# A streaming encoder layer with two kinds of attention: another order of its eight units, a seventeenth weight buffer, and norms of two tiles taken alone

## The chip, the core and the metric

The kernel runs on one core of a Trainium2 chip, in one launch. The metric is the device time of that launch in microseconds, the median of several runs. The core has a matrix engine (PE, or TensorE), a vector engine (DVE, VectorE), a scalar engine for activation functions and scaled copies (ACT, ScalarE), a general engine (POOL, GpSimd) and a queue engine that starts DMA transfers (SP). Each engine works through its own instructions in order and waits on semaphores for the others.

## The reference, cut to what matters

One layer is computed for a prompt of 2048 frames of width 1024 and for 8 running streams ("samples") with 16 new frames and 512 cached frames each:

```python
h, gate = adaln_modulate(x, c, norm_g, w_ada, b_ada)           # rms norm, scale and shift
qa, ka, va, za, qb, kb, vb, zb, ga, gb = split(h @ w_in)       # 512 columns each, ga and gb 1024
qa, ka = rope(qa, pos), rope(ka, pos)
# A, "diff attention", 4 heads of two 64-wide components, mask by chunks of 64 frames
p = softmax(where(mask, q @ k.T / 8, -inf));  oa = (p[0] - lam * p[1]) @ v
# B, "stick breaking", 8 heads of 64, strictly causal
log_a = log_sigmoid(z) + reverse_cumsum(log_sigmoid(-z)) - log_sigmoid(-z);  ob = exp(log_a) @ v
# merge
oa = rms_norm(oa, subln_g) * (1 - lam_init)                    # over each head's 128 columns
ya = (oa * silu(za)) @ w_branch_a
yb = (ob * silu(zb)) @ w_branch_b
y = rms_norm(x + gate * ((sigmoid(ga) * ya + sigmoid(gb) * yb) @ w_out), final_g)
```

The outputs are y for prompt and samples, and the new keys and values of both attentions.

## The kernel before

**Tiles and units.** The prompt is 16 tiles of 128 frames (t = 0 to 15, NT = 16); the 8 x 16 sample frames are one more tile, t = NT. The attention is cut into eight *units*, each with 128 columns of q, k, v and z: four units of kind 0, "A", one head of diff attention each, and four of kind 1, "B", two heads of stick breaking each. In this text A0 is the first A unit, B3 the last B unit. Unit u has h = u // 2 and kind = u % 2, so they run A0 B0 A1 B1 A2 B2 A3 B3.

**What a unit does.** `prepare_unit(u)` loads the unit's columns of w_in, takes their sum of squares, and splits them, scaled, into two fp16 numbers each (high and low part). An A unit holds four weight buffers of 4 KB per partition for that, a B unit eight, since the columns of the merge gates ga and gb are projected in B units (`GATES`). The buffers come from a list `free`. Then, for each tile: `project` does 24 matmuls of 512 columns for q, k, v and z (L423), and in B units 24 more for the gate columns (L495); `transpose_qk` turns q and k; `scores` does the score matmuls (L647, L648, and L651 for a mask), up to 512 keys to a bank of PSUM. An A tile then takes a softmax for its two components (`softmax_pair`): maximum and scaled copy on DVE (L545), Exp on ScalarE, difference of the two on DVE (L594), a cast on ScalarE (L287), the rest on DVE (L292). A B tile takes Sigmoids on ScalarE, scans on DVE (L607, L655), products on POOL (L629), a cast on ScalarE (L561) and the rest on DVE (L562). A DMA transposes the weights, and PE multiplies them with the values (L702 to L704 for A, L706 and L707 for B). For A units a sum of squares of each output tile goes into `osums`, for the norm of oa. The outputs go to DRAM (o_d), as do z (z_d) and the gate columns (g_d). The work of the sample tile is cut into pieces (`spare`) that are strewn over the following units.

**What sets the order.** The program writes the order by hand: `line` is the list of all projection pieces; while it emits the attention of step n, `take` and `interleave` add projection pieces so that projections stay LEAD = 5.0 tiles ahead of attention, weighed by `duration(t)`. The multiplication with the values comes PV_LAG = 2 steps after the scores, and `ripe` holds some of these back at the start of a unit and for tile 15 of an A unit. `prepare_unit(u + 1)` is called at the last step of unit u - 1 and its pieces (`back`) run beside the attention of unit u, so at that time the buffers of a unit in use, of one being used up and of one in preparation are taken. A tile scheduler then orders the instructions of each engine. All Exp and Sigmoid calls go through `act` (L120), which keeps them in program order on ScalarE; where the function changes, ScalarE loads another table (ACT_TABLE_LOAD, shown under the same line).

**The last unit and the last phase.** During unit 7 the weights of the branches are cut (`branch_weight`), and near its end `early_work` does the first part of the last phase: `inputs` of tiles 0 and 1 and the branches of tile 0. The last phase does for each tile: `inputs(t)` loads o, z and the gates, multiplies o by z on POOL (L1230), by Sigmoid of z and, for the A half, by the norm of each head on DVE; takes Sigmoids of the gates; then sum of squares, scale and split. `branches` (L1262) multiplies with the two branch weights and the gates on DVE (L1264) and POOL (L1266), and `output` (L1399) with w_out; its product m is made on DVE (L1403) and added to x on POOL (L1407). The norms of all 16 prompt tiles are one tile `orms` of 64 columns (16 tiles x 4 heads), computed once by twelve small DVE instructions in `rsqrt` (L233 to L246) when `early_work` first calls `inputs`.

Of the kernel before, what the change touches and what calls it, by code (L numbers as in the profile page):

```python
# [16 lines left out]
F32 = mybir.dt.float32  # L17
# [8 lines left out]
P = 128  # L26
# [6 lines left out]
NT = SEQ // P  # L33
# [24 lines left out]

GATES = [(u // 2 * 512, u % 2 * 512) for u in range(8)]

# [50 lines left out]
def layer_kernel(ctx: ExitStack, tc: tile.TileContext, a: dict):  # L111
# [59 lines left out]
    ps = ctx.enter_context(tc.tile_pool(name="ps", bufs=2, space=bass.MemoryType.PSUM))  # L171
    tiny = ctx.enter_context(tc.tile_pool(name="tiny", bufs=6))
    unit = ctx.enter_context(tc.tile_pool(name="unit", bufs=2))
# [130 lines left out]
    def prepare_unit(u):  # L304


        h, kind = u // 2, u % 2
        U = dict(h=h, kind=kind, u=u, w=[], wg=[], bufs=[])
# [434 lines left out]
    def sample(U, dec, fixed):  # L743
# [77 lines left out]
        def values():  # L821
            po = bank("s")
            n = 128 // heads
            for c in range(heads):
                cols = slice(c * n, c * n + n)
                T.matmul(po[:, cols], wn[:, c, :], box["s"][:, 256 + c * n : 256 + c * n + n], start=True, stop=False)
                for r in range(2):
                    for j in range(4):
                        for i in range(4):
                            T.matmul(po[i * 32 : i * 32 + 32, cols], wz[c][:, j, 2 * i + r, :], box[nv, i][:, r * 4 + j, cols],  # L830
                                     start=False, stop=(r == 1 and j == 3))
            o = dec.tile([P, P], F32, tag="o", name="o", bufs=2)
            S.activation(out=o, in_=po[:, 0:P], func=AF.Identity, scale=box["jobs"][0]["r"] if kind == 0 else 2.0 ** -STICK)
# [90 lines left out]
    def ripe(k, n):  # L924

        t = steps[k][1]
        if n >= len(steps) or n <= len(P0_STEPS) or 3 < t < NT and not (t == NT - 1 and steps[k][0] % 2 == 0):
            return True
        return sum(duration(t) for _, t in steps[k + 1 : n]) >= (1.0 if t == NT - 1 else 1.5)
# [261 lines left out]
    (gts,) = buffers_of_4k("gt", 1)  # L1191
    free += buffers_of_4k("wb", 8)
    whole = sum(duration(t) for _, t in steps)
# [12 lines left out]
    L = {}  # L1206
# [8 lines left out]
    def inputs(t):  # L1215
# [8 lines left out]
        begun.append(t)  # L1224
        r = L["orms"][:, 4 * t : 4 * t + 4] if t < NT else rsqrt(osums[:, NT, :], 4, P, tiny, "rA")
        for n in range(2):
# [79 lines left out]
    def early_work():  # L1306
# [4 lines left out]
        def first(t):  # L1311
            if "orms" not in L:
                L["orms"] = rsqrt(osums[:, 0:NT, :].rearrange("p t h -> p (t h)"), 4 * NT, P, con, "orms")
            states[t] = inputs(t)
            if t == tiles[0]:
                turned(states[t])
# [43 lines left out]
    with ExitStack() as c2:  # L1360
# [17 lines left out]
        def gate_rows(i, n):  # L1378

            pg = bank("t")  # L1380
            gsm = s2.tile([P, 512], F32, tag="sg", name="gsm", bufs=2)
            load(out=gsm[0:9, :], in_=gate_d[:, n * 512 : (n + 1) * 512])
# [3 lines left out]
        def output(t, st):  # L1386
            box = {}

            def half(j):
# [7 lines left out]
                for yi, wi in ((0, 0), (0, 1), (1, 0)):  # L1397
                    for k in range(KT):
                        T.matmul(po, st["y"][:, yi * 8 + k, :], wo[j * 4 + k // 2][:, wi, k % 2, :], start=(n == 0), stop=(n == 3 * KT - 1))  # L1399
                        n += 1  # L1400
                m = s2.tile([P, 512], F32, tag="sg", name="m", bufs=2)
                if t < NT:
# [77 lines left out]
```

## Time and profile before

| | |
|---|---|
| runs | 2287.53, 2288.26, 2289.09 us; median 2288.26 |
| the profiled execution | 2285.48 us; its span 2283.7 us |
| instructions | 40470 |
| PE busy | 2085.1 us, 91% of the span |
| PE weight loads busy | 1110.4 us, 49% |
| DVE busy | 1611.5 us, 71% |
| ScalarE busy | 1482.6 us, 65% |
| POOL busy | 688.1 us, 30% |
| last value matmul of the last unit | 1763.3 us |

Times within the profiled execution count from the start of its span. A busy engine is one with an instruction under way; matmuls overlap, so a group's busy time is not the sum of single durations. Rows name the line of the code, the engine, the operation and the tiles it writes and reads, with buffer numbers left out. "L120" is the helper `act`, so its rows are told apart by their tiles. "idle before" is time in which the engine had nothing to do ahead of these instructions, with what ended it.

### The profile page before, as it was taken

Reading aid. Unit: us, or ns where it says so; the run is one execution under the profiler, and the core shown is the slowest. Engines: PE = TensorE matmul, PEld = TensorE weight load, DVE = VectorE, ACT = ScalarE, POOL = GpSimd, SP = SyncE. Lnnn points to the kernel's source line nnn. Section 1 sums busy time; section 2 is a strip of 40 time slices with the busy share of each in tenths; the row PEclk is TensorE's granted clock in tenths of the full one; section 3 lists DMA queues with packets and bytes.
Section 4 is the critical chain, followed back from the end, with each engine's and each line's share of the span. In section 5 each row is a group of like instructions: output and inputs, shape, how many; then the busy total and the mean of one; then the engine's idle time right before and its main releaser. Section 6 shows DMA issues by size and latency. Waiting matters only on the chain. (4 is left out here: it accounts for less than half of the span.)

```text
span 2283.7 us, 40470 instructions
## 1 busy us (share of the span) xinstructions
PE 2085.1 (91%) x14478; PEld 1110.4 (49%) x14478; DVE 1611.5 (71%) x3507; ACT 1482.6 (65%) x2952; POOL 688.1 (30%) x559
## 2 busy tenths in 40 slices
PE   4997999999999999899999989999986799888997
PEld 2554554555555455455545555555543444444443
DVE  4668767789875778987577898776777656565554
ACT  3877677787876777786677777666776544444431
POOL 1522012355301335530032553012344232232321
PEclk7999999999999999999999999999997899999998
DMA  8667658697875778876566886757687989788652
GB/s 295 211 212 187 163 131 220 148 221 155 206 169 124 170 154 199 177 179 131 128 172 142 204 183 154 153 140 163 151 179 173 295 228 262 202 220 211 188 150 65
DMA packets 763754, 411.92 MB, mean 180 GB/s; under 512 B 524986, under 2 KB 708586, under 8 KB 763040
## 3 DMA queue, kind: packets, MB, share of 16 engines
q1 hardware_dynamic: 762474, 408.86, 72.6%
q8 instruction: 113, 1.85, 0.3%
q14 instruction: 89, 0.73, 0.1%
q10 hardware_dynamic: 1078, 0.48, 0.1%
HBM read 211.53 MB, written 72.91 MB: 125 GB/s over the span
## 5 line engine op out<-in xcount | busy, mean ns | idle before, releaser
L423 PE MATMUL ps_mm<-wb,hs 128*128 128x512 f16 x1836 | 460.7, 382 | 0.6 <-DVE v L292 0.5
L629 POOL TENSOR_TENSOR sc_p<-sc_p,sc_n 128x1024 f32<-128x1024 f32 (+8 forms) x160 | 278.1, 1742 | 459.2 <-DVE sc_n L607 451.6
L423 PEld LDWEIGHTS <-hs 128*128 128x128 f16 x2928 | 256.1, 98 | 226.9 <-issue 6.8
L607 DVE TENSOR_TENSOR_SCAN sc_n<-ps_s,sc_n,zero_t 128x512 f32<-128x512 f32 x192 | 245.3, 1278 | 64.4 <-ACT ps_s L120 62.2
L423 PE MATMUL ps_mm<-wa,hs 128*128 128x512 f16 x1092 | 279.4, 380 | 0.0
L647 PE MATMUL ps_s<-k,qst 128*128 128x512 f16 (+3 forms) x640 | 225.9, 354 | 38.3 <-DVE sc_n L607 30.1
L120 ACT ACTIVATE sc_p<-ps_s,usc 128x512 f32<-128x512 f32 (+3 forms) x320 | 202.0, 631 | 85.8 <-PE ps_s L648 55.1
L495 PE MATMUL ps_mm<-wa,hs 128*128 128x512 f16 x1020 | 257.0, 379 | 0.0
L562 DVE TENSOR_TENSOR sc_n<-sc_p,sc_n 128x1024 f16<-128x1024 f32 (+7 forms) x160 | 197.9, 1242 | 41.3 <-ACT sc_n L561 41.2
L648 PE MATMUL ps_s<-k,qst 128*128 128x512 f16 (+3 forms) x640 | 226.2, 354 | 0.0
L1399 PE MATMUL ps_o<-wo,wb 128*128 128x512 f16 x816 | 199.5, 401 | 24.7 <-DMA wb<-wa 22.0
L706 PE MATMUL ps_o<-v,wt 128*128 128x128 f16 x1008 | 175.6, 226 | 27.6 <-DMA wt<-sc_n 27.5
L495 PEld LDWEIGHTS <-hs 128*128 128x128 f16 x1632 | 140.2, 98 | 119.0
L120 ACT ACTIVATE ps_s<-ps_s,usc 128x512 f32<-128x512 f32 (+3 forms) x320 | 193.7, 605 | 0.0
L561 ACT CAST sc_n<-sc_p 128x1024 f16<-128x1024 f32 (+7 forms) x160 | 138.5, 870 | 49.2 <-POOL sc_p L629 49.1
L707 PE MATMUL ps_o<-v,wt 128*128 128x64 f16 x1008 | 158.5, 198 | 0.0
L495 PE MATMUL ps_mm<-wb,hs 128*128 128x512 f16 x612 | 155.9, 379 | 0.0
L706 PEld LDWEIGHTS <-wt 128*128 128x128 f16 x1008 | 99.2, 102 | 102.7 <-DMA wt<-sc_n 38.0
L1399 PEld LDWEIGHTS <-wb 128*128 128x128 f16 x816 | 82.1, 102 | 130.4 <-DMA wb<-wa 26.1
L457 POOL TENSOR_TENSOR rot<-pr,rope 128x256 f32<-128x256 f32 x68 | 63.1, 928 | 247.1 <-ACT pr L437 193.3
L437 ACT ACTIVATE pr<-ps_mm,usc 128x512 f32<-128x512 f32 (+1 forms) x136 | 86.5, 636 | 67.4 <-PE ps_mm L423 67.1
L545 DVE TENSOR_SCALAR_CACHE_REDUCE sc_n<-ps_s,usc 128x512 f32<-128x512 f32 (+3 forms) x148 | 99.0, 669 | 42.4 <-PE ps_s L648 28.2
(336 smaller groups left out, 4346.7 us busy)
## 6 DMA issues: line engine op xcount, KB each, us to landing
hs<-hT_d SPq DMA_DIRECT2D x122, 512.0 KB, 4.2
g_d<-gt SPq DMA_DIRECT2D x68, 256.0 KB, 3.4
out_dram<-pr SPq DMA_DIRECT2D x204, 64.0 KB, 1.8
wa<-g_d SPq DMA_DIRECT2D x25, 512.0 KB, 6.7
wide<-in_w_ada_dram SPq DMA_DIRECT2D x12, 1024.0 KB, 8.4
wa<-in_w_in_dram SPq DMA_DIRECT2D x44, 256.0 KB, 4.7
z_d<-pr SPq DMA_DIRECT2D x136, 64.0 KB, 2.7
o_d<-o SPq DMA_DIRECT2D x136, 64.0 KB, 2.7
```

Source lines behind the costliest of these rows:

```text
L120: i = S.activation(**kw)
L423: T.matmul(box["p"], box["h"][:, hi, k, :], U["w"][k][:, wi, :], start=(n == 0), stop=(n == 3 * KT - 1))
L495: T.matmul(box["g"][:, 0:gw], box["h"][:, hi, k, :], U["wg"][k // per][:, k % per, wi, :], start=(j == 0), stop=(j == 3 * KT - 1))
L561: S.copy(out=hi, in_=src)
L562: V.tensor_tensor(out=lo, in0=src, in1=hi, op=ALU.subtract)
L607: V.tensor_tensor_scan(out=dst[:, lo : lo + n][:, ::-1], data0=src[:, 0:n][:, ::-1], data1=zero_t[:, 0:1].to_broadcast([P, n]), initial=fi ...
L629: G.tensor_tensor(out=p[:, 0:m], in0=p[:, 0:m], in1=n[:, 1 : m + 1], op=ALU.mult)
L647: T.matmul(p[:, 0:n], qst[:, c, :], kk[:, c, 0:n], start=True, stop=False)
L648: T.matmul(p[:, 0:n], qst[:, 2 + c, :], kk[:, c, 0:n], start=False, stop=not diag)
L706: T.matmul(po[:, c * P : (c + 1) * P], wt[:, wj, :], vt[:, c, :, :], start=first, stop=False)
L707: T.matmul(po[:, c * P : c * P + 64], wt[:, nb + wj, :], vt[:, c, 0, :], start=False, stop=last)
L1399: T.matmul(po, st["y"][:, yi * 8 + k, :], wo[j * 4 + k // 2][:, wi, k % 2, :], start=(n == 0), stop=(n == 3 * KT - 1))
```

## The change

The order of the units is written out. It is A0 B0 A1 B1 B2 A2 B3 A3, so two B units are neighbours in the middle and the last unit is an A unit. A ninth buffer in the pool `wb` gives seventeen weight buffers in all, as B1 and B2 hold eight each at the same time. To make room for it, three small pools lose a buffer each: `tiny` (small columns) 6 to 5, the samples' output `o` 2 to 1, and m in `output` 2 to 1 (tag "sg", which the samples' gate row `gsm` shared; that row now uses a tile of the tag "dks"). As the last unit is now an A unit, the sums of squares that `orms` needs come last: `inputs` of the first two tiles of the last phase takes the norms of its own tile alone (4 columns, twelve small instructions each), and `orms` is computed by the first call of `inputs` after these.

```diff
-GATES = [(u // 2 * 512, u % 2 * 512) for u in range(8)]
+ORDER = [(0, 0), (0, 1), (1, 0), (1, 1), (2, 1), (2, 0), (3, 1), (3, 0)]
+GATES = [(h * 512, kind * 512) for h, kind in ORDER]
...
-    tiny = ctx.enter_context(tc.tile_pool(name="tiny", bufs=6))
+    tiny = ctx.enter_context(tc.tile_pool(name="tiny", bufs=5))
...
     def prepare_unit(u):
-        h, kind = u // 2, u % 2
+        h, kind = ORDER[u]
...
-            o = dec.tile([P, P], F32, tag="o", name="o", bufs=2)
+            o = dec.tile([P, P], F32, tag="o", name="o", bufs=1)
...
     def ripe(k, n):
         t = steps[k][1]
-        if n >= len(steps) or n <= len(P0_STEPS) or 3 < t < NT and not (t == NT - 1 and steps[k][0] % 2 == 0):
+        if n >= len(steps) or n <= len(P0_STEPS) or 3 < t < NT and not (t == NT - 1 and ORDER[steps[k][0]][1] == 0):
             return True
...
-    free += buffers_of_4k("wb", 8)
+    free += buffers_of_4k("wb", 9)
...
     def inputs(t):
...
-        r = L["orms"][:, 4 * t : 4 * t + 4] if t < NT else rsqrt(osums[:, NT, :], 4, P, tiny, "rA")
+        if t in tiles[0:2] or t == NT:
+            r = rsqrt(osums[:, t, :], 4, P, tiny, "rA")
+        else:
+            if "orms" not in L:
+                L["orms"] = rsqrt(osums[:, 0:NT, :].rearrange("p t h -> p (t h)"), 4 * NT, P, con, "orms")
+            r = L["orms"][:, 4 * t : 4 * t + 4]
...
         def first(t):
-            if "orms" not in L:
-                L["orms"] = rsqrt(osums[:, 0:NT, :].rearrange("p t h -> p (t h)"), 4 * NT, P, con, "orms")
             states[t] = inputs(t)
...
-            gsm = s2.tile([P, 512], F32, tag="sg", name="gsm", bufs=2)
+            gsm = dec.tile([P, 8, P], F32, tag="dks", name="dks", bufs=4).rearrange("p j n -> p (j n)")[:, 0:512]
...
-                m = s2.tile([P, 512], F32, tag="sg", name="m", bufs=2)
+                m = s2.tile([P, 512], F32, tag="sg", name="m", bufs=1)
```

Three places in the order of the instructions show what moves. Lines in the changed kernel are numbered 1 to 6 higher than before.

The first is ScalarE near the end of the last unit, where the early inputs stand. ps_mm<-hs is the Sigmoid of z, wb or wa onto itself the Sigmoid of a gate. Before, in B3, Sigmoids of scores (sc_p, ps_s from ps_s) stand around them:

```order
L561 CAST sc_n<-sc_p 128x896
L120 ACTIVATE sc_p<-ps_s,usc_18059 128x512
L120 ACTIVATE ps_s<-ps_s,usc_18059 128x512
L120 ACTIVATE ps_mm<-hs_149 128x512 x2
L120 ACTIVATE wb_2118<-wb_2118 128x1024
L120 ACTIVATE wa_137<-wa_137 128x1024
L561 CAST sc_n<-sc_p 128x1024
```

After, in A3, Exps of scores (sc_p, sc_n with their row sums l) stand around them:

```order
L121 ACTIVATE sc_n,l<-sc_n,nm 128x768
L121 ACT_TABLE_LOAD
L121 ACTIVATE ps_mm<-hs_149 128x512 x2
L121 ACTIVATE wa_140<-wa_140 128x1024
L121 ACTIVATE wb_2120<-wb_2120 128x1024
L288 ACTIVATE sc_n<-sc_p,r 128x1024
L288 ACTIVATE sc_n<-sc_p,r 128x640
L275 ACTIVATE junk,uacc<-hs_148 128x1024
L121 ACTIVATE ps_mm<-hs_149 128x512 x2
L121 ACTIVATE wa_142<-wa_142 128x1024
L121 ACTIVATE wb_2116<-wb_2116 128x1024
L121 ACT_TABLE_LOAD
```

The Sigmoids of both tiles' inputs now stand between two table loads, ahead of Exps that are still to come.

The second is ScalarE where B1 ends and the next unit begins (ob is B1's output, L437 and L438 the evacuation of a projection, gt a gate's columns). Before, A2's first Exp comes behind a table load:

```order
L688 ACTIVATE ob<-ps_o,usc_7919 128x128
L450 ACTIVATE qbuf_182<-rot,sq_10637 128x256
L287 ACTIVATE k_11291<-rot,sq_10637 128x2x64
L120 ACT_TABLE_LOAD
L120 ACTIVATE sc_p,l<-sc_p,nm 128x128
```

After, B2's first Sigmoids come there, with no load:

```order
L689 ACTIVATE ob<-ps_o,usc_7920 128x128
L499 ACTIVATE gt_2111<-ps_mm,usc_10663 128x512
L562 CAST sc_n<-sc_p 128x1024
L689 ACTIVATE ob<-ps_o,usc_7920 128x128
L121 ACTIVATE sc_p<-ps_s,usc_10663 128x128
```

B2's projections with their gate columns have taken the place of A2's beside the end of B1.

The third is DVE at the norms of all tiles (rs_q, rs_i, rs_t, rs_w and orms; osums are the sums of squares). Before, they stand in the middle of B3, among the weights of scores:

```order
L620 TENSOR_TENSOR sc_n<-sc_p,sc_n 128x2x384
L233 TENSOR_SCALAR rs_q<-osums 128x64
L235 TENSOR_SCALAR rs_i<-rs_q 128x64
L237 TENSOR_SCALAR orms<-rs_i 128x64
L240 TENSOR_TENSOR rs_t<-orms 128x64
```

After, they stand at the start of the last phase, among the scale of tile 0's merged branches (sy, iy) and its split (wb_2122):

```order
L234 TENSOR_SCALAR rs_q<-osums 128x64
L226 TENSOR_SCALAR sy<-sc_e 128x2
L236 TENSOR_SCALAR rs_i<-rs_q 128x64
L1286 TENSOR_TENSOR iy<-sy,s_w_19266 128x1
L238 TENSOR_SCALAR orms<-rs_i 128x64
L241 TENSOR_TENSOR rs_t<-orms 128x64
L1270 SCALAR_TENSOR_TENSOR wa_142<-ps_mm,iu,wa_142 128x512
```

They moved from the last unit to the first output tile of the last phase.

## The prediction

> **What bounds the kernel now.** I read the page's slices first (each digit is a fortieth of the span, 57 us; tenths busy; PEclk the granted TensorE clock).
>
> ```profile
> PE   4997999999999999899999989999986799888997
> DVE  4668767789875778987577898776777656565554
> PEclk7999999999999999999999999999997899999998
> ```
>
> PE is the busy engine from the second slice on, with one hole, the 31st and 32nd slice (1713 to 1827 us), where the clock falls too. Next, the stages: I took from the timeline the times at which PE issues the first score matmul (L647) of each unit, the last projection and the last value matmul; B3's three are these.
>
> ```profile
> 1523.59 0.22 PE L647 MATMUL ps_s<-k,qst 128*128 128x128 f16 x1
> 1687.33 0.60 PE L495 MATMUL ps_mm<-wb,hs 128*128 128x512 f16 x2
> 1763.14 0.19 PE L707 MATMUL ps_o<-v,wt 128*128 128x64 f16 x1
> ```
>
> Between such times I asked for each engine's busy time. The rows are A1, B1, A2, B2, A3, then B3 up to its last projection matmul, B3's rest up to its last value matmul, and the first us of the last phase.
>
> ```profile
> core 0: us, PE busy (x) PEld busy (x) DVE busy (x) ACT busy (x) POOL busy (x), PEclk, DMA share, GB/s
> 529.20:710.70 181.50, 175.28 (x1250) 96.16 (x1249) 139.28 (x372) 129.75 (x288) 39.69 (x44) 1.00 0.71 169
> 710.70:933.00 222.30, 211.61 (x1511) 113.23 (x1510) 170.91 (x255) 170.30 (x327) 87.75 (x60) 1.00 0.76 173
> 933.00:1114.90 181.90, 175.52 (x1250) 96.13 (x1249) 140.99 (x373) 124.68 (x279) 40.90 (x45) 1.00 0.65 151
> 1114.90:1341.50 226.60, 216.05 (x1511) 114.77 (x1510) 171.34 (x256) 171.89 (x330) 89.39 (x61) 0.98 0.74 169
> 1341.50:1523.60 182.10, 175.42 (x1254) 96.69 (x1253) 142.30 (x385) 122.99 (x275) 41.28 (x46) 1.00 0.66 152
> 1523.60:1687.90 164.30, 162.06 (x1091) 85.05 (x1090) 122.79 (x194) 117.94 (x229) 52.11 (x33) 1.00 0.68 158
> 1687.90:1763.30 75.40, 46.80 (x389) 27.42 (x387) 62.01 (x78) 52.81 (x85) 36.26 (x19) 0.75 0.87 187
> 1763.30:1822.00 58.70, 44.89 (x220) 21.76 (x218) 37.49 (x84) 28.58 (x45) 18.59 (x17) 0.83 1.00 284
> ```
>
> While projections last, PE is 95 to 99% busy. In an A stage it idles 6.2 to 6.7 us, in a B stage 10.6 to 10.7; B3's 75 us without projections idle 28.6 and run at 0.75 of the clock. That last stretch is the hole. The waits in it (window 1687.9 to 1763):
>
> ```profile
> PE ps_o L706 <- DMA wt<-sc_n: 17.8, 9, 5.6
> PE ps_s L647 <- DVE sc_n L607: 9.6, 8, 4.2
> ```
>
> PE waits for weights that DVE and the transposing DMA finish, and for DVE's scans to free score banks. The B stages' idle time sits at their ends, beside the projections of an A unit:
>
> ```profile
> 900.00:950.00 50.00, 41.05 (x383) 23.87 (x382) 47.68 (x75) 40.42 (x82) 29.94 (x22) 1.00 0.87 183
> ```
>
> DVE is nearly full there (95%) and PE loses 9 us.
>
> **The change: what moves.** PE's work stays what it was; it moves between stages. A back-to-back run gives the spacing of projection matmuls:
>
> ```profile
> 1605.37 2.32 PE L423 MATMUL ps_mm<-wb,hs 128*128 128x512 f16 x10
> ```
>
> Ten take 2.32 us; nine spacings and one length of 0.38, so 0.216 us each, 5.2 us for an A tile (24) and 10.3 for a B tile (48, with the gate). Projections run five tiles ahead, so a stage holds tiles 5 to 16 of its own unit and 0 to 4 of the next. A's stage has 12x24 + 5x48 = 528 of them, B's 696, the last B3's 576. After: B1 followed by B2 has 816, A3 as last unit 288. So 288 matmuls, 62.1 us of PE, leave the last unit and are done before it starts.
>
> Term 1, the start of the last unit. From 529.2, A1, B1 (now with five B2 tiles), B2, A2, B3. A stage 181.5 to 182.1; B stage the mean of the two rows, 224.5; B1 gets 5x24x0.216 = 25.9 more, of which 8 fit into the 9 us that PE idles in the row above, since an A tile's work beside B's end becomes a B tile's: 242.4. Sum 529.2+181.5+242.4+224.5+182+224.5 = 1584.1, where it was 1523.6: +60.5. Bounds: if nothing of the idle is filled and B2 after B1 starts badly, +8; if B2 also loses the idle time it has after A2 now, -8.
>
> Term 2, A3 with its projections. B3's 164.3 minus 62.1 is 102.2. DVE is nearer to being the limit than in other A stages (142 us of DVE work in A3's row, against some 125 of PE in the whole unit: 62.2 of projections and the row's 175.4 - 528x0.216 = 61.4 of attention), so I add 3: 105. Bounds 100 (only the shorter work) and 115 (PE at the 82% of that row for half of it).
>
> Term 3, A3's rest, against 75.4. The instructions of a tile (by line and form, the first three in A3's, the last two in B3's stage):
>
> ```profile
> L545 DVE TENSOR_SCALAR_CACHE_REDUCE sc_n<-ps_s,usc 128x512 f32<-128x512 f32 x28 | 20.9, 746 | 10.1 <-PE ps_s L648 7.7 <-PE ps_s L651 2.2
> L594 DVE SCALAR_TENSOR_TENSOR sc_p<-sc_n,r,sc_p 128x1024 f32<-128x1024 f32 x10 | 13.6, 1364 | 0.0
> L292 DVE SCALAR_TENSOR_TENSOR sc_n<-sc_p,r,sc_n 128x1024 f16<-128x1024 f32 x10 | 13.8, 1382 | 0.5 <-ACT sc_n L287 0.5
> L607 DVE TENSOR_TENSOR_SCAN sc_n<-ps_s,sc_n,zero_t 128x512 f32<-128x512 f32 x47 | 60.1, 1279 | 17.6 <-ACT ps_s L120 16.9
> L562 DVE TENSOR_TENSOR sc_n<-sc_p,sc_n 128x1024 f16<-128x1024 f32 x20 | 28.3, 1413 | 5.5 <-ACT sc_n L561 5.5
> ```
>
> DVE per full tile: A 8x0.746 + 2x1.364 + 2x1.382 = 11.5 and about 1 of small ones, B 8x1.279 + 4x1.413 = 15.9 and 0.3: a ratio of 0.77. 75.4x0.77 = 58. Three things lengthen it: table changes, ScalarE's queue and the norms. Their durations:
>
> ```profile
> L120 ACT ACT_TABLE_LOAD x15 | 19.2, 1283 | 0.3
> L120 ACT ACTIVATE ps_mm<-hs 128x512 f32<-128x512 f32 x6 | 3.5, 615 | 5.2 <-DVE hs L1236 4.0 <-DVE wa L1264 1.2
> L120 ACT ACTIVATE wa<-wa 128x1024 f32<-128x1024 f32 x3 | 3.1, 1079 | 0.0
> L274 ACT ACTIVATE junk<-hs 128x1024 f16<-128x1024 f32 x3 | 3.2, 1072 | 5.3 <-DVE hs L1232 5.3
> L287 ACT ACTIVATE sc_n<-sc_p,r 128x1024 f16<-128x1024 f32 x10 | 11.5, 1151 | 5.4 <-DVE sc_p L594 5.4
> L233 DVE TENSOR_SCALAR rs_q<-osums x2: 170/174/179, 1549.1 to 2127.1; 128x64 f32<-128x64 f32 x1, 128x4 f32<-128x4 f32 x1
> ```
>
> ScalarE must change its table between Exp (A) and the Sigmoids of the first two tiles' inputs, which B3's Sigmoids never asked for: twice before the last exponentials. Those (tiles 14 and 15) stand in ScalarE's queue behind the inputs of tiles 0 and 1. What stands between is two tables 2.6, Sigmoids 4x0.615 + 4x1.079 = 6.8, two casts of 1024 and 640 elements 1.15 and some 0.8, a sum of squares 1.1: 12.4. DVE has 6.8 of its own meanwhile, tile 15's scores 8x0.746 = 6.0 and some 0.8 for the first input's product, so it waits 5.6. The norms of tiles 0 and 1 are 24 small DVE instructions of some 0.17 (the last row's shape of 4 columns), 4.1, of which I take 2.4, since part falls into those waits. Together 58 + 5.6 + 2.4 = 66. Bounds 54 (DVE alone, ratio 0.72 without the small ones) and 78 (no gain, tables added).
>
> Term 4, the norms of the other tiles: 12 instructions on 64 columns, 0.18 by the last row, 2.2. They were hidden in the middle of B3 (at 1549); now DVE does them in the last phase's start, after A3's last sum of squares, between tile 0's scale and its split. PE idles 13.8 us in the first 58.7 of that phase (last row of the stages), so I take about half, 1.2; the bounds are 0 and 4, the upper end if the wait for the last output is not covered by tile 0's own chain, which waits for the same matmuls.
>
> At nothing, the smaller pools first. In the last phase the product m passes from DVE to POOL:
>
> ```profile
> L1407 POOL TENSOR_TENSOR x<-m,x 128x512 f32<-128x512 f32 x34 | 48.1, 1416 | 135.2 <-DVE m L1403 92.8 <-DVE m L1406 18.6 <-DVE rA L244 6.8
> L1230 POOL TENSOR_TENSOR hs<-hs,hs 128x512 f32<-128x512 f32 x34 | 45.3, 1351 | 100.2 <-DMA hs<-o_d 65.2 <-issue 30.5 <-DMA hs<-z_d 4.5
> ```
>
> With one m, DVE may write the second half's only after POOL's addition of the first, 1.4 us, but 24 matmuls (5.2 us) lie between the two, and the row shows POOL waiting for m, 92.8 us in all. Without that cover it would be 1.4 us for each of 17 tiles, 24. The single o is used once per unit of samples, some 45 us apart. The seventeenth buffer serves B2's preparation while B1 holds eight; its extra splits and squares (about 10 us of DVE) stand in B1's stage beside 242 us of PE.
>
> Sum: last value matmul at 1584.1+105+66 = 1755.1 instead of 1763.3, -8.2; +1.2; -7.0. The profiled execution took 2285.48 (span 2283.7 and 1.8 around it), so 2278.5; the runs' median is 2288.26, 2.8 above it, and the forecast stands against it: 2281.
>
> On the tables, the row comes first: the switch in the last phase.
>
> ```profile
> 1825.69 0.19 ACT L274 ACTIVATION_READ_ACCUMULATOR junk<-wb 128x1 f32 x1
> 1825.89 1.28 ACT L120 ACT_TABLE_LOAD   x1
> 1827.20 0.60 ACT L120 ACTIVATE ps_mm<-hs 128x512 f32<-128x512 f32 x1
> ```
>
> It stops ScalarE from 1825.88 to 1827.20, 1.3 us. The Trainium skill ("ScalarE: Activation LUTs", section "What ACT_TABLE_LOAD costs") gives the same 1283 ns for the load, but adds a drain of about 1380 ns for every switch; the trace shows none. By that rule the two switches in the tail and the third right behind it would cost some 4 us more (an estimate from that page), and the sum would be -3.
>
> **The rivals.** One: A3's end is no shorter than B3's. For it speaks that A's weights pass DVE, ScalarE, DVE, ScalarE, DVE one after the other, with the table switches and inputs in between; against it, that such a chain did not slow the A stages (6.7 us idle at most). Term 3 is then 73 and the time 2288, no change. A switch that cost twice the row's 1.3 us, with three of them at the end of A3 and right behind it, would add 3.9 and give 2285, also no change; as the row shows no such thing I give it 4 in 100. Two, slower: ScalarE's Sigmoid of tile 1's z waits for its load, which can start only when POOL has multiplied tile 0, and the last exponentials wait behind it, with nothing left for PE. The row on L1230 above shows POOL waiting for loads of o 65.2 us in 34 instructions, and the waits put the longest of them at 12.9:
>
> ```profile
> POOL hs L1230 <- DMA hs<-o_d: 65.2, 10, 12.9
> ```
>
> Above 7 us beyond the sum the gain is gone; at 12.9 the time is 2294. Against it: in B3 the same Sigmoid came without a wait, right behind the sum of squares of the tile before:
>
> ```profile
> 1726.09 1.16 ACT L120 ACTIVATE ps_mm<-hs 128x512 f32<-128x512 f32 x2
> ```
>
> Three, better: B1's end keeps PE full, A3's DVE runs on without the ScalarE wait (term 3 at 58, term 1 at 1580): 2269.
>
> **How the numbers follow.** Chances: forecast 0.48, better 0.12, no shorter end 0.2, dear switches 0.04, slower 0.16. Two runs of this kernel differ by about 0.2% (4.6 us) before one can tell. Faster 0.60, same 0.24, slower 0.16. The forecast alone would lie in 2272 to 2288. The range reaches over the rivals and leaves out a little at each end: 2267 to 2295. The terms' bounds (+-8, -5/+10, +-12), taken as independent, make about +-16 and agree with it.
>
> **What would show it.** A3 starting at 1584 and B1 lasting 242: term 1. PE over 95% busy at B1's end. From A3's first score to its last value matmul 171 us: terms 2 and 3; a rest near 75 is rival one. ScalarE idle before a Sigmoid on hs with exponentials behind it is rival two. The stretch from last value matmul to the end at 520 to 522 us (520.4 before). I would be wrong if B2 after B1 took much longer than 224.5, or the last phase's tiles were spaced wider.

## The result, and the profile after

The changed kernel is slower: 2298.05 us (median of 5 runs, 2293.41 to 2306.68) against 2287.53 before. The ratio is 1.0052, with an interval of 1.0036 to 1.0069. The profiled execution took 2293.41 us, its span is 2291.6.

The page's slices of the changed kernel, as those shown of before:

```profile
PE   4997999998999999999989999998996789989997
PEclk9998999999999999999999999999997899999999
```

The hole is still there (7, 8 in the clock, 6, 7, 8 for PE). The stages, cut as before at the first score matmul of each unit (now L648): A1, B1, B2, A2, B3, then A3 up to its last projection matmul, A3's rest up to its last value matmul, and the first us of the last phase:

```profile
core 0: us, PE busy (x) PEld busy (x) DVE busy (x) ACT busy (x) POOL busy (x), PEclk, DMA share, GB/s
535.09:717.25 182.16, 175.17 (x1250) 96.20 (x1249) 141.23 (x373) 131.16 (x291) 40.68 (x45) 1.00 0.72 172
717.25:970.68 253.43, 242.10 (x1647) 127.22 (x1646) 181.69 (x281) 183.81 (x346) 75.11 (x49) 0.98 0.72 156
970.68:1189.40 218.72, 210.91 (x1520) 112.94 (x1518) 167.09 (x247) 160.63 (x306) 86.02 (x60) 1.00 0.80 176
1189.40:1370.59 181.19, 175.22 (x1250) 96.20 (x1248) 140.58 (x373) 124.63 (x279) 40.84 (x45) 1.00 0.67 155
1370.59:1590.60 220.01, 211.96 (x1511) 113.39 (x1510) 170.01 (x257) 167.47 (x321) 87.55 (x60) 1.00 0.77 171
1590.60:1696.50 105.90, 98.92 (x711) 54.52 (x710) 95.40 (x265) 78.48 (x186) 39.18 (x41) 0.98 0.73 168
1696.50:1767.60 71.10, 47.43 (x368) 29.37 (x366) 54.42 (x131) 49.14 (x85) 10.39 (x9) 0.78 0.59 129
1767.60:1826.30 58.70, 39.90 (x197) 20.08 (x195) 37.43 (x86) 27.75 (x46) 16.67 (x16) 0.85 0.96 277
```

Three things can be read from it. A1 begins 5.9 us later than before (535.1 against 529.2), in a part where the order of the units is still the old one. From A1's first score to the last value matmul it takes 1232.5 us, where before took 1234.1 and the forecast was 1225.9. And from the last value matmul to the end it takes 524.0 instead of 520.4; PE idles 18.8 us of the first 58.7 there, before 13.8. So 5.9 - 1.6 + 3.6 = 7.9 us, the difference of the two spans. How much of each belongs to the change was not to be told from two traces; for that the experiments were made.

(A correction to the words on the kernel above: `prepare_unit(u + 1)` is called at the first step of unit u's attention, not at the last step of the unit before.)

### The profile page after: what moved, and what is told of

Read it like the earlier page. It is cut to its first block, busy times and chain, and to the rows that moved or that the text cites. A ratio compares the mean times of both kernels' runs of the same rounds, so it can differ in the third digit from the quotient of the medians.

```text
span 2291.6 us, 40547 instructions
## 1 busy us (share of the span) xinstructions
PE 2082.4 (91%) x14478; PEld 1112.3 (49%) x14478; DVE 1616.5 (71%) x3529; ACT 1485.8 (65%) x2954; POOL 678.1 (30%) x559
## 5 line engine op out<-in xcount | busy, mean ns | idle before, releaser
L424 PE MATMUL ps_mm<-wb,hs 128*128 128x512 f16 x2142 | 546.0, 382 | 4.2 <-DVE qbuf L452 3.5
L496 PE MATMUL ps_mm<-wa,hs 128*128 128x512 f16 x1122 | 285.5, 379 | 0.0
L648 PE MATMUL ps_s<-k,qst 128*128 128x512 f16 (+3 forms) x640 | 225.8, 354 | 42.2 <-DVE sc_n L608 25.2
L1403 PE MATMUL ps_o<-wo,wb 128*128 128x512 f16 x816 | 193.8, 392 | 17.6 <-DMA wb<-wb 13.4
L424 PE MATMUL ps_mm<-wa,hs 128*128 128x512 f16 x786 | 203.5, 381 | 3.6 <-DVE v L293 2.3
L707 PE MATMUL ps_o<-v,wt 128*128 128x128 f16 x1008 | 179.5, 220 | 11.5 <-DMA wt<-sc_n 11.4
L707 PEld LDWEIGHTS <-wt 128*128 128x128 f16 x1008 | 96.1, 98 | 89.4 <-DMA wt<-sc_n 15.3
L496 PE MATMUL ps_mm<-wb,hs 128*128 128x512 f16 x510 | 131.9, 379 | 0.0
L708 PEld LDWEIGHTS <-wt 128*128 128x128 f16 x1008 | 94.9, 98 | 73.5
L703 PE MATMUL ps_o<-v,wt 128*128 128x128 f16 x544 | 107.0, 226 | 25.8 <-DMA wt<-sc_n 25.3
```

Source lines behind the costliest of these rows:

```text
L424: T.matmul(box["p"], box["h"][:, hi, k, :], U["w"][k][:, wi, :], start=(n == 0), stop=(n == 3 * KT - 1))
L496: T.matmul(box["g"][:, 0:gw], box["h"][:, hi, k, :], U["wg"][k // per][:, k % per, wi, :], start=(j == 0), stop=(j == 3 * KT - 1))
L648: T.matmul(p[:, 0:n], qst[:, c, :], kk[:, c, 0:n], start=True, stop=False)
L707: T.matmul(po[:, c * P : (c + 1) * P], wt[:, wj, :], vt[:, c, :, :], start=first, stop=False)
L708: T.matmul(po[:, c * P : c * P + 64], wt[:, nb + wj, :], vt[:, c, 0, :], start=False, stop=last)
```

## The experiments

Sixteen runs were made, each kernel in turn with the kernel before on its chip. A ratio is to the kernel before, with its interval; 0.001 is 2.3 us. The first four below ran on one chip, the four with one pool or two made smaller on a second, the repaired ones with the buffer from the start on a third, the gate row's second run and the repaired ones with a late 17th buffer on a fourth. Across chips the ratios compare better than the medians. The traces are cut in this table at the first score of A1, the first score of the last unit (B3 or A3) and the last value matmul; "rest" is the stretch from the last projection to the last value matmul. Medians are of 5 to 12 runs; the other columns come from one trace each.

| kernel | median us | ratio | A1 at | A1 to last unit | rest | A1 to last value matmul | last phase |
|---|---|---|---|---|---|---|---|
| before | 2286.2 to 2287.7 | 1 | 529.2 | 994.4 | 75.4 | 1234.1 | 520.4 |
| changed | 2298.05 | 1.0052 | 535.1 | 1055.5 | 71.1 | 1232.6 | 524.0 |
| changed, again | 2302.35 | 1.0059 (1.0038 to 1.0081) | 534.7 | 1058.1 | 74.0 | 1239.0 | 531.4 |
| late 17th buffer | 2299.14 | 1.0049 (1.0029 to 1.0068) | 531.2 | 1058.6 | 74.9 | 1238.8 | 527.5 |
| changed, old order | 2295.03 | 1.0038 (1.0026 to 1.0049) | 533.6 | 990.7 | 73.2 | 1230.9 | 526.2 |
| before, smaller pools | 2296.98 | 1.0045 (1.0028 to 1.0063) | 532.2 | 996.7 | 73.3 | 1233.8 | 528.8 |
| before, one m and gate row | 2297.43 | 1.0042 (1.0028 to 1.0056) | 531.1 | 996.3 | 76.3 | 1237.0 | 526.9 |
| before, gate row | 2293.70 | 1.0031 (1.0019 to 1.0043) | 532.6 | 995.6 | 74.4 | 1234.0 | 519.8 |
| the same, again | 2296.23 | 1.0035 (1.0019 to 1.0051) | 529.6 | 995.5 | 74.1 | 1233.6 | 526.4 |
| before, tiny 5 | 2287.43 | 1.0003 (0.9994 to 1.0012) | 534.8 | 997.8 | 74.6 | 1236.1 | 520.8 |
| before, one o | 2284.98 | 0.9999 (0.9989 to 1.0010) | 531.8 | 995.5 | 75.3 | 1236.8 | 518.0 |
| repaired | 2290.35 | 1.0022 (1.0009 to 1.0034) | 532.5 | 1058.3 | 72.3 | 1237.1 | 520.7 |
| repaired, old order | 2290.35 | 1.0016 (1.0002 to 1.0030) | 534.4 | 994.1 | 75.5 | 1236.5 | 519.7 |
| repaired, tile 0 early | 2292.65 | 1.0027 (1.0013 to 1.0040) | 534.6 | 1055.4 | 68.4 | 1229.6 | 526.7 |
| the same, old order | 2298.25 | 1.0056 (1.0038 to 1.0075) | 535.6 | 990.7 | 71.8 | 1229.2 | 530.8 |
| repaired, late 17th | 2289.82 | 1.0009 (0.9998 to 1.0020) | 531.0 | 1056.4 | 74.3 | 1236.2 | 521.4 |
| the same, old order | 2286.05 | 1.0001 (0.9990 to 1.0012) | 533.1 | 992.7 | 72.9 | 1232.7 | 520.0 |
| repaired, late 17th, tile 1 last | 2287.92 | 1.0007 (0.9993 to 1.0020) | 533.3 | 1055.9 | 69.3 | 1230.9 | 523.2 |

### First four: the change again, the buffer, the order, the pools

The changed kernel without an edit:

> The changed kernel once more, as the anchor for the others. In its first trace A1 began at 535.1 us instead of 529.2, 5.9 late, of which 1.5 arose in the first 40 us (loads of w_ada), and 4.4 between 190 and 535 us, where the order of the units is still the old one. Theory 'buffer': the slip after 190 us belongs to the order that seventeen buffers give, so it is there again: 3 to 6 us from 190 us to A1's start. Rival 'chance': it is jitter of loads; A1's start minus the lag at 190 us is then within 1 us of before. Time by both 2293 to 2300; the last phase 523 to 525 us (520.4 before).

Its 2302.35 us confirm the result; over both sets of runs (11) the median is 2299.4. A1 is late again, and the last phase is even longer, 531.4.

The seventeenth buffer only from B1 on:

```diff
-    free += buffers_of_4k("wb", 9)
+    late = buffers_of_4k("wb", 9)
+    free += late[0:8]
+    del late[0:8]
...
+            if t == NT and u == 3:
+                free.extend(late)
             if t == NT and u < 7:
                 back += prepare_unit(u + 1)
```

> The changed kernel, but the seventeenth buffer joins the list only when B1's attention begins, so that the order of the instructions is that of before up to A1. Theory 'buffer': A1 begins at 529 to 531, the time is 4 to 5 us under the changed kernel's (2289 if that is 2293.5). Rival 'chance': A1 begins anywhere from 529 to 536, no difference to the changed kernel beyond 2 us.

A1 began at 531.2, at the edge of what 'buffer' wants, but the time, 2299.14, is only 0.3 us under the changed kernel's 2299.4, and 3.2 under its 2302.35 on the same chip, which the intervals do not separate. By time alone this run does not tell the theories apart. The old order in the changed kernel:

```diff
-ORDER = [(0, 0), (0, 1), (1, 0), (1, 1), (2, 1), (2, 0), (3, 1), (3, 0)]
+ORDER = [(0, 0), (0, 1), (1, 0), (1, 1), (2, 0), (2, 1), (3, 0), (3, 1)]
```

> The changed kernel with the old order A B A B: seventeen buffers, the smaller pools and the norms taken late stay. Theory 'buffer': A1 begins 3 to 6 us late as in the changed kernel, and the time is 4 to 9 us over before's (2291 to 2296, the last phase's part being open). Rival 'chance', with a last phase that is late because A3 ends there: as before, 2286 to 2290.

2295.03: with the old order 8.9 us of the 16.2 that the changed kernel lost on this chip are still there. The smaller pools alone, in the kernel before:

```diff
-    tiny = ctx.enter_context(tc.tile_pool(name="tiny", bufs=6))
+    tiny = ctx.enter_context(tc.tile_pool(name="tiny", bufs=5))
-            o = dec.tile([P, P], F32, tag="o", name="o", bufs=2)
+            o = dec.tile([P, P], F32, tag="o", name="o", bufs=1)
-            gsm = s2.tile([P, 512], F32, tag="sg", name="gsm", bufs=2)
+            gsm = dec.tile([P, 8, P], F32, tag="dks", name="dks", bufs=4).rearrange("p j n -> p (j n)")[:, 0:512]
-                m = s2.tile([P, 512], F32, tag="sg", name="m", bufs=2)
+                m = s2.tile([P, 512], F32, tag="sg", name="m", bufs=1)
```

> The kernel before, with the smaller pools alone (tiny 5, o 1, m 1, gate row in dks). Its order is that of before up to the last phase. Theory 'pools at nothing' (the prediction): last phase 520 to 521 us, time as before within 2 us. Rival 'pools dear': the 3.8 us that the changed kernel loses in the last phase are theirs: 523 to 525 us there, time 2290 to 2292.

2296.98, 10.8 us over before, with a last phase of 528.8. The edits that the prediction booked at nothing cost most of what the whole change costs (a ratio of 1.0045, against 1.0052 and 1.0059). The price even exceeds what 'pools dear' had asked for. This trace shows one thing more: its instructions stand in the order of before up to the last phase, and still A1 begins at 532.2.

### Next four: which of the pools

One m (with the gate row moved, since both shared a tag); the gate row alone; tiny alone; o alone. The edits are the lines above, one or two at a time.

> The kernel before with one buffer for m (and the gate row moved to dks, since it shared m's tag). The three smaller pools together cost 10.8 us (2296.98 against 2286.18), of which the trace shows 8.4 in the last phase (528.8 us instead of 520.4) and the rest before it, where the order of the instructions is the same. Theory 'm': with one m, the second half of tile 0 waits for POOL's late addition (13 us behind m there), DVE stands with it, and the phase stays behind: 6 to 10 us over before, 2292 to 2296, last phase 526 to 529. Theories 'tiny' and 'o': within 2 us of before, 520 to 522.

> The kernel before with the gate row in a dks tile and nothing else; m keeps two buffers. Theory 'm': within 2 us of before, last phase 520 to 522. Rival 'gate row': it takes two of the four dks tiles when the first sample's keys need them, and changes the order of about 70 rows at the start of the last phase; then this costs the 6 to 10 us that the run with one m costs, 2292 to 2296.

> The kernel before with five buffers in the pool of small columns instead of six; no instruction changes its place in any engine's order, only waits and addresses do. Theory 'm': within 2 us of before. Theory 'tiny': it adds waits of DVE in all units, A1 starts at 531 to 533 instead of 529 and B3 at 1527 to 1529, time 2289 to 2295.

> The kernel before with one buffer for the samples' output o, same order of instructions. Theory 'm', and the prediction: used once in some 45 us, so within 2 us of before, 2284 to 2288. Rival 'o': ScalarE waits for the store of the o before, and the samples' pieces behind it are late: 3 us or more over before.

The pool of small columns and o cost nothing that can be measured (2287.43 and 2284.98), as predicted; in their traces every engine's instructions stand in the order of before. With the gate row alone the ratio is 1.0031, with one m beside it 1.0042: some 7 us come with the gate row, and one m adds about 2.5, which is less than the intervals can separate. So 'm' alone falls, and 'gate row' holds for the larger part.

But the profiled execution of the gate row's kernel showed a last phase of 519.8 us, as short as before's, and it was one of its quickest (2288.19 us). So the kernel ran again:

> The kernel before with the gate row in a dks tile, once more, for a second profile. If its profiled execution lies at 2293 or more, the theory 'gate row in the last phase' wants 524 us or more there; the rival 'jitter before it' wants 518 to 521 there and the last value matmul later than 1768. Its place in SP's queue is the suspect: the loads went out at 1774.2 instead of 1763.8 and 1766.9, behind x, with the samples' loads behind them.

This profiled execution took 2291.45 us, less than the 2293 that the expectation named; its last phase is 526.4 long and its last value matmul comes at 1763.3, as early as before's. So here the loss is in the last phase, and it is not the same in every execution. What differs from before, on SP's queue from the last value matmul on (kernel before, then the gate row's second profile; gsm and dks are the gate row, x the pieces of w_out, wb<-wa the transpose that tile 0's output waits for):

```profile
1763.79 0.38 SPq L1382 DMA_DIRECT2D gsm<-gate_d  x1
1766.88 0.34 SPq L1382 DMA_DIRECT2D gsm<-gate_d  x1
1768.18 1.06 SPq L758 DMA_DIRECT2D dk<-in_cache_a_k_dram  x2
1782.74 5.91 SPq L1287 DMA_TRANSPOSE wb<-wa  x1
```

```profile
1770.06 0.38 SPq L1211 DMA_DIRECT2D x<-in_w_out_dram  x1
1770.49 0.74 SPq L1382 DMA_DIRECT2D dks<-gate_d  x2
1771.66 0.43 SPq L758 DMA_DIRECT2D dk<-in_cache_a_k_dram  x1
1773.34 0.38 SPq L1211 DMA_DIRECT2D x<-in_w_out_dram  x1
1773.77 0.47 SPq L758 DMA_DIRECT2D dk<-in_cache_a_k_dram  x1
1784.74 7.20 SPq L1287 DMA_TRANSPOSE wb<-wa  x1
```

The gate row goes out 6.7 us later, behind another load of w_out, with the samples' loads behind it, and the scheduler has put the rows of all five engines in another order for the first tiles. PE's waits in the first 100 us of the last phase (window 1763.3 to 1863.3 in both), before and then in this kernel:

```profile
PE ps_o L1399 <- DMA wb<-wa: 6.1, 1, 6.1
PE ps_o L1399 <- ACT wo L287: 0.7, 1, 0.7
```

```profile
PE ps_o L1399 <- DMA wb<-wa: 8.6, 1, 8.6
PE ps_o L1399 <- ACT wo L287: 4.1, 1, 4.1
PE ps_s L777 <- DMA dk<-in_cache_a_k_dram: 3.4, 2, 2.5
```

PE waits longer for tile 0's transpose, for the split of w_out on ScalarE and for the samples' keys. The fifth output tile (O4) begins 171.0 us after the last value matmul instead of 164.3, and the lag stays.

That these waits are the cost is argued, not shown, for the first, quick execution of the same kernel has them too. There the last value matmul came at 1766.6, the gate row went out 7.5 us later, and PE waited almost as long (window 1766.6 to 1866.6):

```profile
1774.15 0.74 SPq L1382 DMA_DIRECT2D dks<-gate_d  x2
```

```profile
PE ps_o L1399 <- DMA wb<-wa: 8.3, 1, 8.3
PE ps_o L1399 <- ACT wo L287: 3.0, 1, 3.0
PE ps_s L777 <- DMA dk<-in_cache_a_k_dram: 2.5, 2, 1.5
```

O4 began 168.3 us after that last value matmul, 4.0 later than before, and yet the phase took 519.8. What the runs do show is the price of the edit. Of the eight traces with the row in a dks tile (six of them with one m besides) the other seven have last phases of 524.0 to 531.4 us; the seven traces with the row elsewhere and both tiles' inputs early have 518.0 to 521.4. By which of the moved instructions the time is lost, and why not in every execution, stays open.

One m could hold back tile 0's second half in the changed kernel (the products m on DVE, the additions on POOL, and the first thing that POOL did ahead of the first addition):

```profile
1795.29 0.74 DVE L1407 SCALAR_TENSOR_TENSOR m<-ps_o,iy,gate 128x512 f32<-128x512 f32 x1
1827.24 0.74 DVE L1407 SCALAR_TENSOR_TENSOR m<-ps_o,iy,gate 128x512 f32<-128x512 f32 x1
```

```profile
1803.03 1.12 POOL L290 TENSOR_SCALAR wo<-x,s_w 128x1024 f16<-128x1024 f32 x1 [11.32 <-DMA x<-in_w_out_dram]
1822.34 1.27 POOL L1411 TENSOR_TENSOR x<-m,x 128x512 f32<-128x512 f32 x1 [3.32 <-DVE sc_f L221]
1828.07 1.27 POOL L1411 TENSOR_TENSOR x<-m,x 128x512 f32<-128x512 f32 x1 [4.45 <-DVE m L1407]
```

The first m is ready at 1796.0; POOL, whose queue has splits of w_out and the next tile's product ahead, waiting for their loads, adds it only at 1822.3, and the second half's m had to come after 1823.6. But it came at 1827.24, with other work of DVE ahead of it. In the repaired kernel of the next section, which has two m (parts of a wa buffer), POOL is as far behind the first m, ready at 1800.8, and the second comes no sooner, 59.7 us after the last value matmul against 59.6 here:

```profile
1829.32 0.75 DVE L1407 SCALAR_TENSOR_TENSOR wa<-ps_o,iy,gate 128x512 f32<-128x512 f32 x1 [0.44 <-PE ps_o L1403]
```

```profile
1827.11 2.23 POOL L1411 TENSOR_TENSOR x<-wa,x 128x512 f32<-128x512 f32 x1 [6.62 <-DMA x<-in_x_prompt_dram]
```

DVE has 16 semaphore waits at this line, one for each prompt tile, where the repaired kernel has one. They are short, and what DVE stood idle for POOL's addition there is 1.4 us in the whole phase:

```profile
L1407 DVEq EVENT_SEMAPHORE  x16: 21/21/21, 1826.1 to 2281.2; - x16
  POOL x L1411: 1.4, 1
```

So no long wait for m is seen, and a price of one m alone is not shown.

### The repair: two m and the gate row in the seventeenth buffer

In the last phase the seventeenth buffer lies idle. Its two halves became the two m and the gate row:

```diff
-            L["g"], L["u"], (L["y"], L["y16"]) = free[0:4], free[4:6], free[6:8]
+            L["g"], L["u"], (L["y"], L["y16"]), L["m"] = free[0:4], free[4:6], free[6:8], free[8].rearrange("p (f n) -> p f n", f=2)
...
-            gsm = dec.tile([P, 8, P], F32, tag="dks", name="dks", bufs=4).rearrange("p j n -> p (j n)")[:, 0:512]
+            gsm = L["m"][:, n if i == 0 else 1 - n, :]
...
-                m = s2.tile([P, 512], F32, tag="sg", name="m", bufs=1)
+                m = L["m"][:, j, :]
```

> The changed kernel with the two halves of the seventeenth buffer, idle in the last phase, as the two m, and the gate row in them too; the order of the units is the new one, o 1 and tiny 5 stay. Theory 'm and gate row': the last phase, 524 to 531 us in three traces of the new order, comes back to 519 to 522, and the time falls by 6 to 10 us from the changed kernel's (11 runs, median 2299.4) to 2287 to 2293. Rival 'order': the last phase is late because A3 ends it, with norms and inputs; then 524 to 531 and 2295 to 2300 remain.

2290.35 us, 9 less than the changed kernel's 2299.4 (by the ratios, 1.0022 against 1.0052 and 1.0059, 7 to 8 less), and a last phase of 520.7. 'm and gate row' holds, 'order' as the cause of the long last phase falls. The repair undoes both edits at once, and its gate row goes out 137 us ahead of the last value matmul (at 1632.18), while it went out behind it in the kernel before. The wait at the product of m went from sixteen to one:

```profile
L1407 DVEq EVENT_SEMAPHORE  x1: 21/21/21, 2269.5 to 2269.5; - x1
```

The same with the old order of the units:

> The same with the old order A B A B four times. Theory 'm and gate row': last phase 518 to 521, 2283 to 2288, no different from before; the difference to the run with the new order is then what the order itself is worth: by the prediction the new order is 7 us the faster, by the traces so far (from A1's start to the last value matmul 1236.8 on average against 1235.3) 0 to 3 us the slower. Rival 'seventeenth buffer or late norms cost': 2290 or more.

2290.35 as well (ratios 1.0016 and 1.0022). The order is worth nothing here. The time lies 2 us over the expected range, which speaks for the rival 'seventeenth buffer or late norms'; the next runs part these. The repaired kernels with the buffer in the list from B1 on, new and old order:

> The changed kernel with m and the gate row in the seventeenth buffer, and that buffer joins the list only at B1. Theory 'buffer': A1 begins near 531.8 instead of 534.4 (means of seven traces each), 2.6 us off the repaired kernel's 2290.35: 2286 to 2289, the same as before. Rival: no change, 2289 to 2292.

> The same with the old order, for which the seventeenth buffer is then of use only to m and the gate row. Theory 'buffer': 2285 to 2288 and no different from before; the order is worth 0 to 2 us either way. Rival 'late norms': 2290 as with the buffer from the start, as the norms at the start of the last phase are what is left.

With the old order 2286.05, no different from before (0.9990 to 1.0012): the late norms, and whatever else is left of the change there, cost nothing that can be measured. With the new order the time, 2289.82, lies in the range of the rival 'no change', though A1 began at 531.0, as the theory 'buffer' wanted. The two medians across the chips differ by 4.3 us in the old order and 0.5 in the new, but by the ratios the late buffer saves 3.4 and 3.0 us, and 2.3 in the changed kernel (1.0059 against 1.0049); none of the three is clear of its intervals. A1 began at 534.4 us on average in the seven traces that have the buffer from the start (532.5 to 535.6), and at 531.8 in the eleven that do not (529.2 to 534.8). So some 2.6 us come before A1, which fits the ratios.

The new order against the old, by ratio: 1.0022 against 1.0016, and 1.0009 against 1.0001. It brings nothing, and may cost some 1 to 2 us; that is not settled.

### A3's end

The wait that the prediction had not seen stands on DVE in the changed kernel, in the window 1696 to 1768 (the second of the groups in this window is PE's, the third ScalarE's):

```profile
DVE hs L1242 <- POOL hs L1236: 6.4, 1, 6.4
PE ps_o L703 <- DMA wt<-sc_n: 16.8, 5, 5.7
ACT sc_p L121 <- DVE nm L575: 9.0, 3, 4.7
```

And in DVE's timeline:

```profile
1743.19 0.15 DVE L575 TENSOR_REDUCE nm<-mx 128x2 f32<-128x8 f32 x1
1749.74 1.12 DVE L1242 SCALAR_TENSOR_TENSOR hs<-ps_mm,rA,hs 128x128 f32<-128x128 f32 x4 [6.39 <-POOL hs L1236]
1750.78 0.16 DVE L585 TENSOR_TENSOR l<-l 128x2 f32<-128x2 f32 x1
1752.01 2.48 DVE L595 SCALAR_TENSOR_TENSOR sc_p<-sc_n,r,sc_p 128x1024 f32<-128x1024 f32 x2
```

DVE stands 6.4 us before tile 1's input (L1242), which waits for POOL's product, which waits for its load; behind it stand the last tile's sums and weights (L585, L595), for which ScalarE's row sums are ready at 1748.0, so that they are 2.8 us late by it. The load could only go out when tile 0's split on DVE had read the same buffer, at 1741.0, and stood behind the transpose of that split in SP's queue:

```profile
1743.28 0.78 SPq L1219 DMA_DIRECT2D hs<-o_d  x1
```

So two kernels took tile 1's inputs out of the unit's end, to behind the last value matmul, with the new and with the old order:

```diff
-        ... [lambda t=t: first(t) for t in tiles[0:2]]
+        ... [lambda t=t: first(t) for t in tiles[0:1]]
...
+    states[tiles[1]] = inputs(tiles[1])
     with ExitStack() as c2:
```

> The first of these two with only tile 0's inputs in A3's end; tile 1's come behind the last value matmul. In the changed kernel DVE waits 6.4 us there for POOL's product of tile 1 (whose load comes late), with the last softmax queued behind it. Theory 'tile 1 in the way': A3's rest falls from 71 to 75 us to 65 to 68; the last phase grows by 0 to 6, as tile 1 is later; net 0 to 6 us faster than with both early. Rival 'chain': A's own chain of DVE, ScalarE and DMA is the limit; the rest stays at 71 to 75.

> The old order with only tile 0's inputs early. In B3's end nothing of the attention is queued behind tile 1's product for long. Theory 'tile 1 in the way' speaks of A3 alone: the rest stays at 73 to 76 us and the last phase grows by 0 to 6, so 0 to 6 us slower than the old order with both early. Rival: the rest falls here too, and tile 1's inputs cost either order the same.

The rest fell to 68.4 (72.3 with both early), and the last phase grew by 6.0, to 526.7: in these traces more given back than won. The medians, 2292.65 against 2290.35, agree, within their intervals. In the old order the rest fell too (75.5 to 71.8), so the rival holds there: tile 1's inputs cost either order's end some 4 us. But the old order lost 7.9 us in all (2298.25 against 2290.35), with a last phase of 530.8, so with tile 1's inputs late the new order is 5.6 us the faster of the two, at the edge of the intervals. What an order is worth may depend on which early inputs go with it. The third kernel kept them early, but last among the early pieces, with both repairs and the new order:

```diff
-            ... [lambda t=t: first(t) for t in tiles[0:2]] + [lambda i=i: early(i) for i in range(5)]
+            ... [lambda: first(tiles[0])] + [lambda i=i: early(i) for i in range(5)] + [lambda: first(tiles[1])]
```

> The new order with the two repairs, and tile 1's inputs as the last of the early pieces, so that the last softmax is ahead of them on DVE. Theory 'tile 1 in the way': A3's rest 66 to 70 us instead of 72 to 75, the last phase 520 to 524, together 0 to 5 us under the version with both early: 2282 to 2288, perhaps under before. Rival: what the end gains the last phase gives back, as with tile 0 alone early: 2287 to 2292.

The rest is 69.3 and the wait of DVE for POOL's product is gone from the window; the largest of DVE's waits that is left there:

```profile
DVE wb L1272 <- PE ps_mm L1270: 4.3, 2, 2.5
```

The last phase took 523.2, 1.8 longer than in the kernel it was made from. 2287.92, 1.9 us under that kernel's 2289.82 but within the intervals of both, and no different from before. No version tried here beats the kernel before.

## Why the prediction was wrong, point by point

**The step that failed first: "At nothing, the smaller pools first".** The four edits that stand there cost 10.8 us by themselves in the kernel before. Most of that, 7 to 8 us (1.0031 and 1.0035), comes with the gate row's move, which had no term at all: it was read as a change of address, while it changed the order of the instructions on every engine in the last phase, its own two loads among them. The working for m took its cover, 24 matmuls between the two m and a POOL that waits for m, from sums over the whole phase. At the phase's start it does not hold, as POOL is 26 us behind the first m. But that is so with two m as well, so no trace shows it to be the cost, and one m beside the gate row adds 2.5 us by ratio, within the intervals. Both undone, the kernel is 7 to 9 us faster. The prediction had named a sign of this, output tiles spaced wider: O4 begins 175.7 us after the last value matmul in the changed kernel, 164.3 before.

**Term 1, the start of the last unit: right in its sum, by luck.** From A1 to A3's first score the forecast was 1054.9; seven traces of the new order have 1055.4 to 1058.6. It came out of errors that cancel. B1 took 253.4 instead of 242.4: PE was indeed full at its end, as forecast, but it still idles 11.3 us of the stage, most of it now in the unit's first 105 us, and its busy time of 242.1 is 4.6 over the 211.6 + 25.9 worked out, at a clock of 0.98. B2 (218.7), A2 (181.2) and B3 (220.0) took less than forecast.

**The base of term 1: not.** The forecast counted from 529.2, A1's start in the one trace of before. The kernels whose instructions stand in the order of before that far began A1 at 529.6 to 534.8. The trace of before was early by some 3 us there, which is not the change's, and for which the 2.8 us that the forecast added for the runs' median about make up; the buffer in the list from the start added 2.6, which had no term.

**Term 2, A3 with its projections: right.** 105.3 to 106.9, forecast 105.

**Term 3, A3's rest: mis-sized, and this is the first rival's case.** Forecast 66, measured 71.1 to 74.9; the rival had 73. The size that failed is first the ratio of 0.77. It was worked out for one tile and put on the whole rest of B3, as if A3's rest held the same tiles. It holds more: the last part of the softmax of five tiles (11 to 15), where B3's holds that of three and one piece of a fourth. This is seen in the lengths of DVE's weights, in B3's rest (1687.9 to 1763.3 before) and then in A3's (1696.5 to 1767.6 in the changed kernel). (B3's nine pieces of 1024 are eight of tiles 13 to 15, in two heads, and one more; A3's six are two of tile 15 and one each of tiles 11 to 14, and the keys of tile 12 end in a piece of 640, of tile 11 in one of 512; four traces of the new order have the same pieces.)

```profile
L562 DVE TENSOR_TENSOR sc_n<-sc_p,sc_n 128x1024 f16<-128x1024 f32 x9 | 13.4, 1485 | 0.0
```

```profile
L595 DVE SCALAR_TENSOR_TENSOR sc_p<-sc_n,r,sc_p 128x1024 f32<-128x1024 f32 x6 | 7.6, 1279 | 0.0
L595 DVE SCALAR_TENSOR_TENSOR sc_p<-sc_n,r,sc_p 128x512 f32<-128x512 f32 x1 | 1.2, 1217 | 0.0
L595 DVE SCALAR_TENSOR_TENSOR sc_p<-sc_n,r,sc_p 128x640 f32<-128x640 f32 x1 | 0.9, 880 | 0.0
```

DVE was busy 54.4 us there, 0.88 of the 62.0 in B3's rest; the working's 0.77 and 2.4 for the norms make 50. The terms for the tables were about right, and the drain that the Trainium skill adds ("ScalarE: Activation LUTs", section "What ACT_TABLE_LOAD costs") is not seen here either: in A3's end the load fills 1716.50 to 1717.78 between two instructions, without a gap.

```profile
1716.29 0.19 ACT L121 ACTIVATION_READ_ACCUMULATOR sc_n<-sc_n,nm 128x1 f32 x1
1716.50 1.28 ACT L121 ACT_TABLE_LOAD   x1
1717.79 1.12 ACT L121 ACTIVATE ps_mm<-hs 128x512 f32<-128x512 f32 x2
```

What was missed beside the ratio is tile 1's input on DVE, 6.4 us of standing, 2.8 of them with the last softmax ready; it came in place of the 5.6 that DVE was to wait for ScalarE. The second rival had named the late load, but put the wait on ScalarE before a Sigmoid; the Sigmoids came without a wait, and it was DVE's product behind POOL's that stood, with the last softmax behind it. Taken out or put last, the rest went down by 4 to 5 us, but the last phase gave back 2 to 6, so much of the gain was not to be had that way, and a rest of 68.4 and 69.3 is still above the forecast.

**Term 4, the late norms: at the lower end.** Forecast 1.2 with bounds of 0 and 4; with the repairs the last phase is 519.7 to 521.4 with the norms in it, 520.4 before.

Put together, the forecast's -7.0 became about 0 to +2 for the order with its norms, +7 to +9 for m and the gate row, and some +2 to +3 for the buffer from the start. The first of these was tested with both tiles' inputs early alone, and the last is clear of chance only in A1's start.

## What to carry to other kernels

A tile moved to another pool is not only another address: compare the order of the instructions on every engine before and after. The two smaller pools that left every order as it was cost nothing here; the moved row, which changed it in the last phase, cost 7 to 8 us. And look at a cover at its worst moment, which here was the start of a phase, not at its mean. When a stretch is scaled by the work of one tile, count the tiles that it holds after the change. Work that is pulled early into the tail of another stage takes a place in each engine's queue: look for the engine on which its slowest input is awaited with the tail's own last steps behind it. And where two edits of a change are meant to be free so that a third can pay, run the free ones alone first.

## What the runs showed that was not expected

Kernels with the same instructions in the same order began A1 between 529.2 and 534.8 us in single traces, and one kernel showed a last phase of 519.8 us in one profiled execution and 526.4 in another, on two chips, another kernel 524.0 and 531.4. A difference of a few us between two traces, place by place, is therefore not yet a price; the prediction's base of 529.2 was one such draw.
